# Centring v through its weights: group means on VectorE, and transposes in place of the gated layer's centring products

## The chip, the cores and the metric

The kernel runs on one core of a Trainium2 chip. The metric is the device time of one execution in microseconds (us); the median of several timed runs is given. One further execution was recorded by the hardware profiler, and all rows below come from that one. In the rows PE is TensorE's matmul, PEld its weight load, DVE is VectorE, ACT ScalarE, POOL GpSimd and SP SyncE; L258 is line 258 of the kernel.

## The reference, cut to what matters

A trunk of two layers over 1024 positions with width 1024, all in float32. The first layer multiplies the normalised input h by one wide matrix `e_w_in` and cuts the product into pieces for two mixers, an RWKV-7 time mixing and a chunked spatial gate. The change touches the gate's v alone, which is normalised over each group of 64 columns:

```python
def layernorm(x, g, b, eps):
    mu = jnp.mean(x, axis=-1, keepdims=True)
    var = jnp.mean(jnp.square(x - mu), axis=-1, keepdims=True)
    return (x - mu) * lax.rsqrt(var + eps) * g + b

v = layernorm(v.reshape(bsz, t_len, B_GROUPS, B_GROUP_DIM), ...)   # 8 groups of 64
...
mixed = jnp.einsum('gts,bcsgd->bctgd', w, v) + b_s...              # causal w, chunks of 128
return u * mixed.reshape(bsz, t_len, B_WIDTH)
```

The second layer is a sliding-window attention; a final normalisation follows.

## The kernel before

The wide matrix is walked in column blocks of 128, 25 of them after four that are done at the start, in the order of the list `ORDER`: 21, 5, 1, 9, **17**, 6, 2, 10, 22, 13, 25, 7, 3, 11, 23, **18**, 14, 26, 24, **19**, 15, 27, **20**, 16, 28. Columns 17 to 20 are v. Each column is computed for two halves of 512 positions by `gproj`, with float32 split in two parts: 8 blocks of the inner dimension times three products, so 24 matmuls of 128x512 for a half, all of tile `pproj`.

The generator `stream` does this walk. For each column it first issues the two DMAs (`wfetch`, L247, on SP's queue, 256 KB each) of the next column's weights into two of three `wraw` buffers, then the 24 matmuls of the first half, then the evacuation of that half, then `wsplit`: ScalarE rounds each raw half to `whi` (L257) and GpSimd subtracts it to `wlo` (L258); both are held behind the last matmul issued so far (`paced`). Then comes the second half.

TensorE's instructions stand in an order written out by hand: the function `drive` takes turns among several generators (scan, prep, solve, fronts, tail, ada, stream), each of which yields the latency that it expects before it wants to go on. The time mixing needs long chains that go between TensorE, ScalarE and VectorE (`solve`, `prep`, `scan`); the stream's 128x512 matmuls fill the time between. Instructions of the other engines are put in order by a scheduler from their priorities and from its own estimates of time; those of the time mixing have raised priority, those of `stream` have not. On the chip each queue runs in the order so found.

A half of v goes through `v_evac` (ScalarE copies the `pproj` result to `vT`, L992) and then through `gm_tail`: four products on TensorE, `vT` block times the constant `cblk` (identity minus 1/64 in each 64x64 block), both turn v round to positions on the partitions and take off the mean of each group of 64. ScalarE squares the result (L902), VectorE sums the squares (L904) and GpSimd takes the power -1/2 (L907); VectorE scales (L909); later come the mixing products (`mix`). Eight halves of v, two for each of the columns 17 to 20, go this way.

Of the kernel before, what the change touches and what calls it, by code (L numbers as in the profile page):

```python
# [11 lines left out]
F32 = mybir.dt.float32  # L12
# [3 lines left out]
ALU = mybir.AluOpType  # L16
AX = mybir.AxisListType
# [3 lines left out]
P = 128  # L21
# [84 lines left out]
def tile_kernel(ctx, tc, x, cons, par, rows, ada, ada0, ew, wup, sgw, sgb, ewo, ow, owo, out, dbg=None):  # L106
# [10 lines left out]
    def paced(*ops):  # L117
        for op in ops:
            behind(op, last[0])

    def cost(lhsT, rhs):
        n = math.prod(rhs.shape[1:])
        m = math.prod(lhsT.shape[1:])
        if rhs.dtype == F32R:
            return max(n if n >= 256 else 4 * n, m) / 2400.0
        return max(4 * n, 2 * m, 60) / 2400.0

    def mm(out, lhsT, rhs, **kw):
        clock[0] += cost(lhsT, rhs)
        last[0] = nc.tensor.matmul(out, lhsT=lhsT, rhs=rhs, **kw).ins  # L130

    def transpose(out, in_, ident):
        clock[0] += 512 / 2400.0
        return nc.tensor.transpose(out, in_, ident)  # L134

    V = nc.vector
# [16 lines left out]
    def pg(name):  # L153
        return ps.tile([P, HT], F32, name=name, tag="g", bufs=1)
# [12 lines left out]
    def PC(name, i):  # L167
        return prm[:, COLS[name] + i:COLS[name] + i + 1]

    ident = con[:, CONSTS["ident"]:CONSTS["ident"] + P]  # L170
    cblk = con[:, CONSTS["cblk"]:CONSTS["cblk"] + P]
# [72 lines left out]
    def wfetch(src):  # L244
        raws = [wp.tile([P, 4, P], F32, name="wraw", tag="wraw", bufs=3) for g in range(2)]
        for g in range(2):
            d = nc.sync.dma_start(out=raws[g], in_=src[:, g * 4:g * 4 + 4, :])  # L247
            if clock[0] < 100.0:
                behind(d, start_dma[0])
        return raws  # L250

    def wsplit(raws, pace=True, E=G):
        hi = wp.tile([P, KC, P], F32R, name="whi", tag="whi", bufs=2)
        lo = wp.tile([P, KC, P], F32R, name="wlo", tag="wlo", bufs=2)
        for g in range(2):
            gs = slice(g * 4, g * 4 + 4)
            a = S.activation(hi[:, gs, :], raws[g], AF.Copy)  # L257
            b = E.tensor_tensor(out=lo[:, gs, :], in0=raws[g], in1=hi[:, gs, :].bitcast(F32), op=ALU.subtract)  # L258
            if pace:
                paced(a, b)  # L260
        return hi, lo
# [14 lines left out]
    def gproj(w, half, hs=None):  # L276
        whi, wlo = w
        hhi, hlo = (hs or h)[half]
        pt = pproj("pproj")
        for k in range(KC):  # L280
            mm(pt, lhsT=whi[:, k, :], rhs=hhi[:, k, :], start=(k == 0), stop=False)
            yield 0.0
            mm(pt, lhsT=whi[:, k, :], rhs=hlo[:, k, :], start=False, stop=False)
            yield 0.0
            mm(pt, lhsT=wlo[:, k, :], rhs=hhi[:, k, :], start=False, stop=(k == KC - 1))
            yield 0.0
        return pt
# [7 lines left out]
    def new_h():  # L295
        return [new_hh(half) for half in range(2)]
# [47 lines left out]
    with tc.manual_schedule(engines={nc.tensor.engine}):  # L344
# [37 lines left out]
        def wfirst(i, g):  # L382
            raw = rt.tile([P, 4, P], F32, name="wr", tag="krv", bufs=6)
            tc.keep_in_program_order(nc.sync.dma_start(out=raw, in_=ew[FIRST[i][0]][:, g * 4:g * 4 + 4, :]))
            return raw
# [98 lines left out]
        raws = [wfirst(i, 0) for i in range(4)]  # L484
# [3 lines left out]
    with tc.manual_schedule(engines={nc.tensor.engine, nc.scalar.engine, nc.vector.engine, nc.gpsimd.engine}):  # L488
# [7 lines left out]
        raws = [wfirst(i, 1) for i in range(4)]  # L496
# [42 lines left out]
    gl = gls.enter_context(tc.tile_pool(name="gl", bufs=1, reuse_waits="tile"))  # L539
# [336 lines left out]
    def ghalf(nm, tag, bufs):  # L876
        return gl.tile([P, HT], F32, name=nm, tag=tag, bufs=bufs)

    def gm_consts(j):
        sgwt = gl.tile([P, 2, P], F32, name="sgwt", tag="sgwt", bufs=1)  # L880
        nc.scalar.dma_start(out=sgwt, in_=sgw[:, 2 * j:2 * j + 2, :])
        lnb = gl.tile([P, P], F32, name="lnb", tag="lnb", bufs=1)
        nc.scalar.dma_start(out=lnb, in_=rows[3, j * P:(j + 1) * P].partition_broadcast(P))
        bst = gl.tile([P, P], F32, name="bst", tag="bst", bufs=1)
        for g in range(2):
            nc.scalar.dma_start(out=bst[g * 64:g * 64 + 64, :], in_=sgb[2 * j + g, :].partition_broadcast(64))
        return sgwt, lnb, bst

    def gm_tail(j, half, vT):
        if half == 0:  # L890
            gmc[j] = gm_consts(j)
        sgwt, lnb, bst = gmc[j]
        yield lat("gm_tail1", 2 * j + half)
        if half == 0:
            paced(G.tensor_tensor(out=sgwt, in0=sgwt, in1=tri.unsqueeze(1).to_broadcast([P, 2, P]), op=ALU.mult))
        vn = gl.tile([P, 4, 2, 64], F32, name="vn", tag="vn", bufs=1)
        pv = pg("gvn")
        for i in range(4):
            mm(pv[:, i * P:(i + 1) * P], lhsT=vT[:, i * P:(i + 1) * P], rhs=cblk, start=True, stop=True)
        long[0] -= 1  # L900
        sq = ghalf("gsq", "gt", 3)
        S.activation(sq, pv, AF.Square)  # L902
        st = gl.tile([P, 8], F32, name="gst", tag="gst", bufs=2)
        V.tensor_reduce(out=st, in_=sq.rearrange("p (a d) -> p a d", d=64), axis=AX.X, op=ALU.add)  # L904
        V.tensor_scalar(out=st, in0=st, scalar1=1.0 / 64, scalar2=GMLP_EPS, op0=ALU.mult, op1=ALU.add)
        rs = gl.tile([P, 8], F32, name="grs", tag="grs", bufs=2)
        G.tensor_tensor(out=rs, in0=st, in1=nhalf[:, 0:8], op=ALU.pow)  # L907
        vg = vn.rearrange("p b g d -> p (b g) d")
        V.tensor_tensor(out=vg, in0=pv.rearrange("p (a d) -> p a d", d=64), in1=rs.unsqueeze(2).to_broadcast([P, 8, 64]), op=ALU.mult)  # L909
        yield lat("gm_tail2", 2 * j + half)  # L910
        yield lambda: (j, half) in gated_u
        if half == 0:
            pb = pg("lnb")
            for g in range(2):
                mm(pb[g * 64:g * 64 + 64, 0:P], lhsT=lnb[:, g * 64:g * 64 + 64], rhs=sgwt[:, g, :], start=True, stop=True)
            V.tensor_tensor(out=bst, in0=pb[:, 0:P], in1=bst, op=ALU.add)
            yield lat("lnb", 2 * j + half)
        ut = gated_u.pop((j, half))
        px = pg("mix")
        for i in range(4):  # L920
            for g in range(2):
                mm(px[g * 64:g * 64 + 64, i * P:(i + 1) * P], lhsT=vn[:, i, g, :], rhs=sgwt[:, g, :], start=True, stop=True)
        mx = ghalf("mx", "gt", 3)
        V.scalar_tensor_tensor(out=mx.rearrange("p (b t) -> p b t", t=P), in0=px.rearrange("p (b t) -> p b t", t=P), scalar=PC("sg", j), in1=bst.unsqueeze(1).to_broadcast([P, 4, P]), op0=ALU.mult, op1=ALU.add)
        V.tensor_tensor(out=ut, in0=mx, in1=ut, op=ALU.mult)
        nc.sync.dma_start(out=y0d[:, 4 + j, half * HT:(half + 1) * HT], in_=ut)
        short[0] -= 1
# [77 lines left out]

    ORDER = (21, 5, 1, 9, 17, 6, 2, 10, 22, 13, 25, 7, 3, 11, 23, 18, 14, 26, 24, 19, 15, 27, 20, 16, 28)

    def stream():
        todo = list(ORDER)
        for i in range(4):  # L1010
            if i == 1:
                raws = wfetch(ew[todo[0]])
            pt = (yield from gproj(ws[i], 1)) if i else pt1
            FIRST[i][1](1, pt)
            if i == 1:
                w = wsplit(raws)
        while todo:
            n = todo.pop(0)
            raws = wfetch(ew[todo[0]]) if todo else None
            pt = yield from gproj(w, 0)  # L1020
            yield room[n]
            evac[n](0, pt)
            if todo:
                wn = wsplit(raws)
            pt = yield from gproj(w, 1)
            yield room[n]
            evac[n](1, pt)
            if todo:
                w = wn
        done["h1"] = new_h()  # L1030

    def lat(name, un):
        return LAT.get(name, 0.0) + MORE.get(name, (0.0,) * 8)[un]
# [110 lines left out]
    def out0_thread():  # L1144
# [19 lines left out]
        for b in range(NB):  # L1164
# [22 lines left out]
            if b == NB - 2:  # L1187
# [8 lines left out]
    wes = ExitStack()  # L1196
    threads = [[0, scan_thread(), 0.0, None], [1, prep_thread(), 0.0, None], [1, solve_thread(), 0.0, None], [2, fronts_thread(), 0.0, None],
               [4, tail_thread(), 0.0, None], [5, ada_thread(), 0.0, None], [6, stream(), 0.0, None], [5, wo0_thread(), 0.0, None], [7, out0_thread(), 0.0, None]]

    def drive():  # L1200
# [191 lines left out]
    for n in range(2):  # L1392
        hi, lo = new_hh(n)
        for k in range(KC):
            raw = wp.tile([P, HT], F32, name="wraw", tag="wraw", bufs=3)
# [112 lines left out]
```

## Time and profile before

| what | value |
|---|---|
| median of 3 runs | 1091.95 us (1091.01 to 1092.3) |
| the profiled execution, its own time | 1086.66 us |
| its span, first to last instruction | 1084.8 us |
| its mean granted TensorE clock | 0.988 of full speed |
| busy: PE, PEld, DVE, ACT, POOL | 96%, 77%, 64%, 48%, 34% of the span |

The busy shares are over the whole span, which has stages with different limits: a start up to about 95 us, the first layer's mixers from about 95 to 605 us, and the first output projection and the attention layer after that. Matmuls are pipelined, so the duration of one is longer than the time that it takes up in a row of them; what one takes up is read from start to start. A row of a timeline merges neighbours of one kind (x8 is eight instructions), and what stands in brackets is the engine's idle time just before the row and what ended it.

### The profile page before, as it was taken

How to read it: one execution, taken by the hardware profiler on the slowest of the kernel's cores; microseconds unless marked ns; L12 is line 12 of the kernel's file. 1: busy time of each engine (PE TensorE's matmuls, PEld its weight loads, DVE VectorE, ACT ScalarE, POOL GpSimd, SP SyncE). 2: the span in 40 equal slices, each digit the busy share in tenths (PEclk: the TensorE clock that was granted, in tenths of full speed). 3: DMA queues.
4: the chain of work that ended last, by engine and by line, in shares of the span. 5: the costliest groups of instructions: out<-in, count | busy, mean ns of one | idle time of the engine just before them, and what ended most of it. 6: DMA issues, size and time to landing. Idle time of an engine off the chain costs nothing.

```text
span 1084.8 us, 20721 instructions
## 1 busy us (share of the span) xinstructions
PE 1039.3 (96%) x7887; PEld 834.1 (77%) x7888; DVE 694.0 (64%) x1668; ACT 521.5 (48%) x1247; POOL 370.2 (34%) x483
## 2 busy tenths in 40 slices
PE   6989989998999899999999999999999999999997
PEld 3667767777777677777888787778888888878886
DVE  4355868595868585858433688755565544488753
ACT  4464464544454546454423223336665644486521
POOL 2233323232323233233344100225455544467201
PEclk9989999999999999999999999999999999999998
DMA  9601121212121122212213655411011011251221
GB/s 363 238 18 40 60 79 59 70 50 69 64 86 57 60 68 70 69 53 84 91 61 124 184 183 177 146 45 40 23 37 40 20 40 40 98 165 59 75 81 59
DMA packets 55131, 93.42 MB, mean 86 GB/s; under 512 B 5748, under 2 KB 15988, under 8 KB 55032
## 3 DMA queue, kind: packets, MB, share of 16 engines
q1 hardware_dynamic: 45176, 77.36, 21.5%
q10 hardware_dynamic: 9856, 14.75, 4.2%
q8 instruction: 62, 1.02, 0.4%
q14 instruction: 37, 0.30, 0.1%
HBM read 79.49 MB, written 12.59 MB: 85 GB/s over the span
## 4 chain that ended last, share of the span: by engine, by line
PE 52%; DVE 4%; ACT 2%; issue 1%; DMA 1%; POOL 1%; ACTq 0%; POOLq 0%; DVEq 0%; SPq 0%
PE pproj L130 24%; PE op L130 16%; PE po L130 2%; PE pS L130 2%; PE pT L1319 2%; PE htp L134 1%; PE pM L130 1%; PE py L130 0%; DVE pr L728 0%; DMA wraw<-y0d 0%; PE mix L130 0%; DVE Sx L1305 0%; PE mq L130 0%; PE gvn L130 0%; PE uw L130 0%
## 5 line engine op out<-in xcount | busy, mean ns | idle before, releaser
L130 PE MATMUL pproj<-hi,whi 128*128 128x512 f32 x696 | 281.1, 404 | 0.7 <-ACT vt L1273 0.7
L130 PE MATMUL pproj<-hi,wlo 128*128 128x512 f32 x696 | 280.7, 403 | 0.0
L130 PE MATMUL pproj<-lo,whi 128*128 128x512 f32 x696 | 280.6, 403 | 0.0
L258 POOL TENSOR_TENSOR wlo<-wraw,whi 128x512 fp32r<-128x512 f32 x86 | 114.8, 1353 | 155.2 <-ACT whi L257 154.3
L130 PEld LDWEIGHTS pproj<-hi,whi 128*128 128x128 f32 x696 | 131.4, 189 | 27.8 <-issue 3.6
L130 PEld LDWEIGHTS pproj<-hi,wlo 128*128 128x128 f32 x696 | 131.3, 189 | 26.0 <-issue 2.4
L130 PEld LDWEIGHTS pproj<-lo,whi 128*128 128x128 f32 x696 | 131.5, 189 | 25.0 <-issue 1.7
L130 PE MATMUL op<-wo,whi 128*128 128x512 f32 x256 | 81.1, 397 | 0.1
L257 ACT ACTIVATE whi<-wraw 128x512 fp32r<-128x512 f32 x102 | 59.0, 622 | 37.2 <-issue 13.5
L1309 ACT ACTIVATE Sx<-Sx,nm 128x257 f32<-128x257 f32 (+1 forms) x128 | 62.3, 489 | 27.3 <-DVE nm L1305 25.3
L1305 DVE CUSTOM_DVE_ANT_0 Sx<-pS,bias,nsink 128x256 f32<-128x256 f32 (+1 forms) x128 | 53.5, 463 | 30.0 <-PE pS L130 28.6
L1313 POOL TENSOR_SCALAR Sx<-Sx,rc 128x256 f32<-128x256 f32 (+1 forms) x128 | 60.8, 492 | 25.6 <-DVE rc L1311 23.1
L1325 DVE TENSOR_TENSOR PL<-pT,PH 128x512 fp32r<-128x512 f32 (+1 forms) x64 | 41.6, 655 | 29.7 <-ACT PH L1324 29.2
L944 DVE SCALAR_TENSOR_TENSOR adacc<-araw,cond,adacc 128x512 f32<-128x512 f32 x56 | 48.4, 864 | 19.2 <-DMA araw<-ada 19.1
L130 PEld LDWEIGHTS op<-wo,whi 128*128 128x128 f32 x256 | 47.6, 188 | 11.4 <-ACT whi L257 0.6
L130 PE MATMUL op<-hi,yh 128*128 128x512 f32 (+1 forms) x136 | 51.8, 381 | 0.4 <-ACT yh L1423 0.4
L130 PE MATMUL op<-hi,yl 128*128 128x512 f32 (+1 forms) x136 | 51.7, 380 | 0.4 <-DVE yl L1424 0.4
L130 PE MATMUL op<-lo,yh 128*128 128x512 f32 (+1 forms) x136 | 51.5, 379 | 0.0
L130 PE MATMUL op<-wo,wlo 128*128 128x512 f32 x128 | 50.8, 397 | 0.0
L1324 ACT ACTIVATE PH<-pT 128x512 fp32r<-128x512 f32 (+1 forms) x64 | 35.7, 563 | 17.4 <-PE pT L1319 16.1
L728 DVE TENSOR_TENSOR pr<-Lf,LT 128x2 f32<-128x2 f32 (+14 forms) x120 | 42.2, 352 | 2.4
L225 POOL TENSOR_TENSOR st<-st,nhalf 128x1 f32<-128x1 f32 x16 | 9.6, 601 | 96.7 <-DVE st L224 96.7
(317 smaller groups left out, 2153.2 us busy)
## 6 DMA issues: line engine op xcount, KB each, us to landing
araw<-ada SPq DMA_DIRECT2D x64, 256.0 KB, 2.7
wraw<-ew SPq DMA_DIRECT2D x50, 256.0 KB, 3.0
wraw<-ow SPq DMA_DIRECT2D x36, 256.0 KB, 2.7
adaraw<-ada SPq DMA_DIRECT2D x16, 512.0 KB, 8.4
x<-x SPq DMA_DIRECT2D x8, 512.0 KB, 9.7
woraw<-ewo SPq DMA_DIRECT2D x16, 256.0 KB, 2.9
xr<-x ACTq DMA_DIRECT2D x16, 256.0 KB, 3.8
wraw<-y0d SPq DMA_DIRECT2D x16, 256.0 KB, 3.4
```

What stands on the lines that cost most here:

```text
L130: last[0] = nc.tensor.matmul(out, lhsT=lhsT, rhs=rhs, **kw).ins
L134: return nc.tensor.transpose(out, in_, ident)
L257: a = S.activation(hi[:, gs, :], raws[g], AF.Copy)
L258: b = E.tensor_tensor(out=lo[:, gs, :], in0=raws[g], in1=hi[:, gs, :].bitcast(F32), op=ALU.subtract)
L728: V.tensor_tensor(out=pr[:, 0:nc_, 0:i + 1], in0=Lf[:, i:i + 1, 0:i + 1].to_broadcast([P, nc_, i + 1]), in1=LTt[:, 0:nc_, 0:i + 1], op=ALU ...
L944: op = V.scalar_tensor_tensor(out=acc, in0=raw, scalar=cond[:, k:k + 1], in1=acc, op0=ALU.mult, op1=ALU.add)
L1305: V.tensor_tensor_reduce(out=Sx[:, e, off:2 * P], in0=pS3[:, e, 0:nk], in1=bias[e][:, off:], scale=1.0, scalar=nsink[:, hd:hd + 1], op0=AL ...
L1309: S.activation(pr[:, e, off:2 * P + 1], Sx[:, e, off:2 * P + 1], AF.Exp, bias=nm[:, e:e + 1], scale=-1.0, accum_out=sm[:, e:e + 1])
L1313: G.tensor_scalar(out=pr[:, e, off:2 * P], in0=pr[:, e, off:2 * P], scalar1=rc[:, e:e + 1], scalar2=0.5, op0=ALU.mult, op1=ALU.mult)
L1319: nc.tensor.transpose(pT4[:, kb, e, :], pr[:, e, kb * P:(kb + 1) * P], ident)
L1324: S.activation(PH[:, ks, :], pT2[:, ks, :], AF.Copy)
L1325: V.tensor_tensor(out=PL[:, ks, :], in0=pT2[:, ks, :], in1=PH[:, ks, :].bitcast(F32), op=ALU.subtract)
```

## The change

The mean is taken off the weights in place of the product. The four products of a half become four transposes against the identity. For columns 17 to 20 a new function runs on VectorE over the two raw weight tiles before they are split: for each partition and inner block it sums each group of 64 columns, and subtracts a 64th of that sum in place.

```diff
         for i in range(4):
-            mm(pv[:, i * P:(i + 1) * P], lhsT=vT[:, i * P:(i + 1) * P], rhs=cblk, start=True, stop=True)
+            transpose(pv[:, i * P:(i + 1) * P], vT[:, i * P:(i + 1) * P], ident)
         long[0] -= 1
...
+    def wcentre(n, raws):
+        if 17 <= n < 21:
+            for raw in raws:
+                rg = raw.rearrange("p k (b d) -> p (k b) d", d=64)
+                wm = gl.tile([P, 8], F32, name="wm", tag="wm", bufs=2)
+                V.tensor_reduce(out=wm, in_=rg, axis=AX.X, op=ALU.add)
+                V.scalar_tensor_tensor(out=rg, in0=wm.unsqueeze(2).to_broadcast([P, 8, 64]), scalar=-1.0 / 64, in1=rg, op0=ALU.mult, op1=ALU.add)
+
     def stream():
...
             evac[n](0, pt)
             if todo:
+                wcentre(todo[0], raws)
                 wn = wsplit(raws)
```

`transpose` and `mm` add the same time to `drive`'s clock for a 128x128 float32 block (512/2400 us); `transpose` does not set the matmul behind which `paced` instructions are held. The two new VectorE instructions are not `paced`.

## Rows read from the trace of the kernel before

**Rows 1.** The page: busy time of the engines with its share of the span, and PE's busy share in 40 equal slices of the span (tenths).
```profile
PE 1039.3 (96%) x7887; PEld 834.1 (77%) x7888; DVE 694.0 (64%) x1668; ACT 521.5 (48%) x1247; POOL 370.2 (34%) x483
...
PE   6989989998999899999999999999999999999997
```

**Rows 2.** The page: the chain that ended last, by engine.
```profile
PE 52%; DVE 4%; ACT 2%; issue 1%; DMA 1%; POOL 1%; ACTq 0%; POOLq 0%; DVEq 0%; SPq 0%
```

**Rows 3.** Windows: stretch, its length, then busy time (and instructions) of PE, PEld, DVE, ACT and POOL, granted clock, DMA share, GB/s. The first layer's mixers, and the stretch in which column 18's weights are split.
```profile
95.00:605.00 510.00, 488.71 (x5048) 383.69 (x5048) 346.11 (x801) 243.45 (x552) 165.50 (x135) 0.99 0.23 72
...
385.00:410.00 25.00, 23.82 (x188) 18.51 (x188) 24.00 (x62) 10.94 (x22) 11.80 (x10) 1.00 0.29 86
```

**Rows 4.** The waits of PE between 95 and 605 us, longest first: engine, tile, line, releaser: us in total, times, longest.
```profile
PE pM L130 <- DVE Tq L760: 5.6, 2, 2.9
PE chain L130 <- DVE PA L838: 5.6, 7, 1.7
PE pM L130 <- ACT M L752: 5.6, 3, 2.6
```

**Rows 5.** PE's timeline around the first centring products (`gvn`) and around four transposes (`kb`) a little later: start, us, engine, line, operation.
```profile
182.20 0.39 PE L130 MATMUL pproj<-hi,wlo 128*128 128x512 f32 x1
182.43 1.05 PE L130 MATMUL gvn<-con,vT 128*128 128x128 f32 x8
183.24 0.48 PE L130 MATMUL pproj<-hi,whi 128*128 128x512 f32 x1
...
184.48 0.39 PE L130 MATMUL pproj<-hi,wlo 128*128 128x512 f32 x1
184.72 0.60 PE L134 MATMUL kb<-con,sqk 128*128 128x128 f32 x4
185.07 0.48 PE L130 MATMUL pproj<-hi,whi 128*128 128x512 f32 x1
```

**Rows 6.** Windows, columns as in rows 3: the stretch of rows 5, and one of the stretches at half clock.
```profile
181.00:188.00 7.00, 7.00 (x42) 6.04 (x41) 6.73 (x15) 1.51 (x4) 5.64 (x4) 1.00 0.26 77
195.30:198.70 3.40, 3.40 (x30) 2.47 (x30) 2.40 (x5) 1.83 (x5) 0.00 (x0) 0.50 0.25 77
```

**Rows 7.** Groups of DVE instructions by line and shape: count, then busy us and mean ns of one, then idle time before them.
```profile
L565 DVE TENSOR_REDUCE nsk<-sqk 128x8 f32<-128x512 f32 x8 | 5.5, 683 | 0.1
...
L867 DVE SCALAR_TENSOR_TENSOR bv<-yc,der,bv 128x512 f32<-128x512 f32 x8 | 6.0, 752 | 15.0 <-ACT yc L866 15.0
...
L944 DVE SCALAR_TENSOR_TENSOR adacc<-araw,cond,adacc 128x512 f32<-128x512 f32 x56 | 48.4, 864 | 19.2 <-DMA araw<-ada 19.1
```

**Rows 8.** Timelines of POOL and ACT: the split (`wlo`) of columns 18 and 19, and the evacuation of the first half of each of these columns (`vT`).
```profile
402.46 2.99 POOL L258 TENSOR_TENSOR wlo<-wraw,whi 128x512 fp32r<-128x512 f32 x2
...
498.91 2.53 POOL L258 TENSOR_TENSOR wlo<-wraw,whi 128x512 fp32r<-128x512 f32 x2
...
427.89 0.60 ACT L992 ACTIVATE vT<-pproj 128x512 f32<-128x512 f32 x1
...
517.54 0.60 ACT L992 ACTIVATE vT<-pproj 128x512 f32<-128x512 f32 x1 [0.18 <-PE pproj L130]
```

**Rows 9.** DMA issues of weight columns between 95 and 605 us (KB each, median us to landing), and from SP's timeline the issues of the raw weights of columns 17, 18, 19 and, with one of the next column, 20.
```profile
wraw<-ew SPq DMA_DIRECT2D x45, 256.0 KB, 3.0
...
135.60 0.86 SPq L247 DMA_DIRECT2D wraw<-ew  x2
...
387.94 1.61 SPq L247 DMA_DIRECT2D wraw<-ew  x2
...
471.46 2.84 SPq L247 DMA_DIRECT2D wraw<-ew  x2
...
534.95 11.85 SPq L247 DMA_DIRECT2D wraw<-ew  x3
```

**Rows 10.** Timelines of DVE and PE where column 17's raw weights land.
```profile
140.04 0.75 DVE L314 SCALAR_TENSOR_TENSOR krv<-pproj,prm,krv 128x511 f32<-128x511 f32 x1
...
142.86 0.29 DVE L758 TENSOR_TENSOR Zq<-Zq,pM 128x128 f32<-128x128 f32 x1 [0.64 <-issue]
...
143.79 0.45 DVE L760 STREAM_TRANSPOSE Tq<-Zq 128x256 f32<-128x256 f32 x1
...
142.02 0.73 PE L130 MATMUL pM<-Zq,M 32*32 32x16 f32 x64 [2.60 <-ACT M L752]
...
144.86 0.69 PE L130 MATMUL pM<-Tq,N 32*32 32x32 f32 x32
```

**Rows 11.** Timelines of DVE and PE after column 18's raw weights have landed.
```profile
408.88 0.42 DVE L733 TENSOR_TENSOR ZT<-Tm,rcon 128x256 f32<-128x256 f32 x1
...
413.21 0.69 DVE L621 SCALAR_TENSOR_TENSOR BK<-kkn,tha 64x512 f32<-64x512 f32 x1
416.16 0.75 DVE L867 SCALAR_TENSOR_TENSOR bv<-yc,der,bv 128x512 f32<-128x512 f32 x1 [2.26 <-ACT yc L866]
...
411.73 0.75 PE L130 MATMUL pM<-ZT,Dg 16*32 16x32 f32 x64
...
416.35 0.60 PE L134 MATMUL bkt<-con,BK 128*128 128x128 f32 x4
```

**Rows 12.** DVE's timeline: the first instructions after its idle times behind the landings of columns 19 and 20.
```profile
486.49 0.86 DVE L814 TENSOR_TENSOR Z<-mq,i 64x256 f32<-64x256 f32 x2 [4.76 <-PE mq L130]
...
548.21 0.28 DVE L838 SCALAR_TENSOR_TENSOR PA<-chain,dC,PA 128x64 f32<-128x64 f32 x1 [5.83 <-PE chain L130]
```

## The prediction

> **What bounds the kernel now.** I read first the busy times and the slices of the page: PE is busy 96% of the span, in nearly every slice nine tenths or more, DVE 64% [rows 1]. The chain that ended last has PE with 52%, DVE with 4% [rows 2] (its shares don't fill the span; I take only the order from it). Then the windows: in the 510 us of the first layer's mixers, where the whole change lies, PE is busy 488.71 us and DVE 346.11 us [rows 3]. So PE's idle time there is about 21 us, and what is taken from PE's own work shortens the kernel unless a wait takes its place. PE's waits in that stage show which waits there are: three kinds of 5.6 us each, all in the chains of the time mixing, on DVE's `Tq`, on DVE's `PA` and on ACT's `M` [rows 4]. No wait for `whi` or `wlo` is among the nine that the view lists. So DVE work is cheap where DVE is idle, and it is on PE's path where it stands in front of `Tq`, `PA` or what ACT needs for `M`.
>
> **What the change takes away.** A float32 product of 128x128 is two matmul instructions, a transpose one: the four products of a half are x8, the four transposes of `kb` x4 [rows 5]. What they take up is read from start to start: `gvn` starts at 182.43 and the next `pproj` at 183.24, 0.81 us; `kb` starts at 184.72 and the next `pproj` at 185.07, 0.35 us. From the `pproj` before to the one behind it is 1.04 against 0.59 us, which gives the same difference. Of the same shapes and in the same surroundings a half gains 0.46 us, and eight halves 3.7 us (8 x 0.46 = 3.68). The order on PE should stay, since the hand-written clock counts both alike. A small part could be lost where PE then waits 0.46 us longer for something that doesn't move; with 21 of 510 us idle [rows 3] that is seldom, so I deduct nothing here and let the stalls below stand for it.
>
> [...]
>
> **What it adds.** Eight sums over 128x512 and eight fused multiply-adds over 128x512 on DVE, no DMA and nothing on another engine. The nearest sum takes 0.683 us, the nearest multiply-add from SBUF 0.752 us; one that runs much beside other traffic 0.864 us [rows 7]. A column is two of each: 2 x (0.683 + 0.752) = 2.9 us, at most 3.1 us; four columns 11.5 to 12.4 us. If it all lay on PE's path the change would cost 11.5 - 3.7 = 7.8 us; if none did it would give 3.7 us. Column by column:
>
> - **Splitting later.** `whi` now waits for DVE, and `wlo` behind it. Columns 18 and 19 have their `wlo` done at 405.45 and 501.44, and their first half is evacuated at 427.89 and 517.54 [rows 8]: 22 and 16 us, of which the 24 matmuls of the half take 24 x 0.233 (the spacing of `pproj` in rows 5) = 5.6 us and the interleaved work some more. 3.1 us fits in. What is queued behind a waiting `whi` on ACT are evacuations and the chain's `M` and `Z`; I take zero for it, since the raw weights are there well ahead of the split (column 18's at about 392.5, its `wlo` at 402.46 [rows 8, 9]), and leave what it could do to the slow rival.
> - **Where the sums will stand.** They are not held behind a matmul as the split is, so a scheduler that fills gaps will put them as soon as the raw weights are there: 3.0 us after an issue [rows 9], so at 138.6 to 139.5 us for column 17, 391 to 392.5 for 18, 474.5 to 477 for 19, and from about 538 for 20.
> - **Columns 19 and 20.** DVE is idle 4.76 us before 486.49 and 5.83 us before 548.21 [rows 12]. 2.9 us fit into either: zero, or 2.9 us if they stand ahead of a link of the chain instead.
> - **Column 17.** Right where its weights land, DVE has `krv` at 140.04, then `Zq` (0.64 us idle before it) and `Tq`, which ends at 144.24; PE already waits 2.60 us for ACT's `M` at 142.02, and takes `Tq` at 144.86 [rows 10]. A sum ahead of `Zq` delays `Tq`, whose slack is 0.62 us. Bounds: nothing if all four instructions come behind `Tq`, 2.9 us if all come ahead. The two raw tiles land a microsecond apart, so I expect one instruction to slip ahead: 0.7 us.
> - **Column 18.** DVE is busy 24.00 of the 25 us from 385 to 410 [rows 3], and there the sums push all that follows. `ZT` ends at 409.30 and PE takes it at 411.73; `BK` ends at 413.90 and PE takes it at 416.35 [rows 11]. The slack is 2.43 and 2.45 us, against 2.9 to 3.1: a stall of 0.4 to 0.7 us, of which I take 0.5. Behind that DVE has 2.26 us idle before 416.16 [rows 11], so the delay ends there. Bounds: nothing if they are put behind it, 2.9 us if they find no slack.
>
> **The sum.** -3.7 + 0.7 + 0.5 = -2.5 us. The profiled execution took 1086.66 us, 5.3 us below the median of the runs; the terms are differences inside one execution, so the median moves by as much: 1091.95 - 2.5 = 1089.5 us. Between no stall and 1.5 us of stalls this case runs from 1088.2 to 1089.8 us. A measurement of this kernel tells about 0.2%, that is 2.2 us, from no change; the sum is just beyond it.
>
> **The rivals.**
>
> - **The gain is eaten.** One column's DVE time comes through whole (2.9 us at column 17 or 18), or stalls of 1.5 to 5.9 us in all: -2.2 to +2.2 us, its middle 1091.2 us (-3.7 + 2.9). For it: PE's waits on `Tq`, `PA` and `M` stand close to both landings [rows 4, 10]. Against it: half of the columns meet idle DVE [rows 12].
> - **Slower: VectorE's queue in front of the time mixing.** A sum that is placed ahead of a chain link holds the whole queue, also while it waits for the second raw tile: of column 19's two issues the second comes up to 2.84 us after the first [rows 9]. At 2.9 us for each of columns 17, 18 and 19 it is 8.7 - 3.7 = +5.0 us, 1097.0 us. It decides from 3.7 + 2.2 = 5.9 us of stalls, that is from two columns at full price. Against it: the chains have the higher priority.
> - **The clock falls at the transposes.** A stretch at half clock is 3.4 us at 0.50 [rows 6]; it does 1.7 us of work and so loses 1.7 us. One costs half the gain; two with the 1.2 us of stalls give -3.7 + 3.4 + 1.2 = +0.9 us, 1092.9 us. [...]
> - **More than the sum.** The chains move against the clock's windows, no column stalls, and one stretch at half clock goes: -3.7 - 1.7 = -5.4 us, 1086.6 us.
> - **That the change doesn't do what it says**: that a transpose here takes up as much as a product; the 0.35 us of `kb` [rows 5] leaves next to no room for this, and I count it with the eaten gain.
>
> **How the numbers follow.** The forecast has 42 in 100, the eaten gain 28, slower 18, more than the sum 8, the clock 4. Faster by over 0.2% are the first and the fourth, 50 in 100; within 0.2% the second and the last, 32; slower 18. The range from 1086.5 to 1095.0 us holds all but most of the slow case. The forecast's own range is 1088.2 to 1089.8 us.
>
> **What would show it.** Each `gvn` group should be x4 and take about 0.35 us to the next `pproj`. Right for the costs: a DVE group of eight sums at 0.68 us and eight multiply-adds at 0.75 to 0.86 us; no PE wait on `whi` or `wlo`; PE's wait before the `pM` of 142 us grown by less than a microsecond. It is wrong if the waits of PE on `Tq`, `PA` or `M` grow by more than 1.5 us in all, if ACT waits for DVE at `whi` in front of an evacuation, or if there are more or fewer stretches at half clock than before.

## The result and the profile after

The change made the kernel slower. The median went from 1091.48 us (1090.88 to 1092.3, 4 runs) to 1097.21 us (1096.61 to 1098.73, 4 runs), a ratio of 1.0049 with a 95% interval from 1.003 to 1.0067. The forecast was 1089.5 us, its range ended at 1095.0 us. The profiled execution of after took 1096.61 us. Three of the kernels below had one execution each of 1544.75 to 1677.46 us, at a granted clock of 0.555 to 0.598, which every number here leaves out.

The busy times of the page, then the windows of the first layer's mixers and of the stretch in which column 18 is split (columns as in rows 3), both of after:

```profile
PE 1042.1 (95%) x7856; PEld 833.6 (76%) x7856; DVE 702.1 (64%) x1684; ACT 521.5 (48%) x1247; POOL 369.9 (34%) x483
```

```profile
95.00:605.00 510.00, 483.91 (x4958) 378.20 (x4957) 348.19 (x806) 239.07 (x544) 161.69 (x133) 0.97 0.22 69
385.00:410.00 25.00, 23.71 (x216) 17.48 (x213) 22.18 (x58) 10.97 (x26) 3.60 (x4) 1.00 0.19 54
```

PE is busy 4.8 us less in the same 510 us than in [rows 3] although the work takes longer: it waits more. The granted clock of the stretch is 0.97 where it was 0.99. PE's waits between 95 and 615 us in after, longest first:

```profile
PE pM L130 <- DVE Tq L760: 6.7, 4, 2.9
PE pM L130 <- DVE ZT L733: 6.0, 3, 2.9
PE chain L130 <- DVE PA L838: 4.4, 7, 1.7
PE pM L130 <- ACT N L711: 2.7, 8, 1.0
PE pM L130 <- ACT M L752: 2.3, 2, 1.5
PE pproj L130 <- DVE krv L314: 1.6, 1, 1.6
```

There is no wait on `krv` in before, and for `ZT` one of 0.3 us:

```profile
PE pM L130 <- DVE ZT L733: 0.3, 1, 0.3
```

That on `M` has shrunk from the 5.6 us of [rows 4]; at 190 us `ZT` has taken its place. The gain itself is there. PE's timeline of after at the first centring group:

```profile
184.41 0.39 PE L130 MATMUL pproj<-hi,wlo 128*128 128x512 f32 x1
184.64 0.60 PE L134 MATMUL gvn<-con,vT 128*128 128x128 f32 x4
184.99 0.48 PE L130 MATMUL pproj<-hi,whi 128*128 128x512 f32 x1
```

From `gvn` to the next `pproj` is 0.35 us, where it was 0.81 [rows 5]. When the starts of the same PE instructions in both traces are set side by side, after is 2.1 us ahead at 132 us, 1.7 us behind at 144.86, 6.1 us behind at 192 and 8.4 to 10.9 us behind from 266 us on (times of before). At each of the eight `gvn` groups it catches up by 0.4 to 0.5 us. So most of the loss arises before 270 us, and only its first part where a sum was added.

**The first place** is column 17. DVE's timeline of after, and PE's waits there:

```profile
124.38 0.23 DVE L728 TENSOR_TENSOR pr<-Lf,LT 128x45 f32<-128x45 f32 x1
125.70 0.69 DVE L1013 TENSOR_REDUCE wm<-wraw 128x8 f32<-128x512 f32 x1 [1.09 <-DMA wraw<-ew]
126.30 0.68 DVE L569 TENSOR_TENSOR sqk<-kt,nik 128x512 f32<-128x512 f32 x1
126.90 0.19 DVE L729 TENSOR_REDUCE LT<-pr 128x5 f32<-128x45 f32 x1
...
127.99 1.77 DVE L1014 SCALAR_TENSOR_TENSOR wraw<-wm,wraw 128x512 f32<-128x512 f32 x1
129.68 0.25 DVE L728 TENSOR_TENSOR pr<-Lf,LT 128x50 f32<-128x50 f32 x1
...
133.48 0.50 PE L130 MATMUL pproj<-hi,whi 128*128 128x512 f32 x1 [1.57 <-DVE krv L314]
137.58 0.75 PE L130 MATMUL pM<-ZT,Dg 16*32 16x32 f32 x64 [1.53 <-DVE ZT L733]
```

The first sum is in DVE's queue between two links of the `pr`, `LT` chain that leads to `ZT`, and holds the queue 1.09 us for its raw weights; the multiply-add behind it takes 1.77 us. PE waits 1.57 us for `krv` and 1.53 us for `ZT`.

**The second place** is at 190 us, where no sum is near. DVE's timeline of after, then of the kernel before:

```profile
189.12 0.68 DVE L904 TENSOR_REDUCE gst<-gsq 128x8 f32<-128x512 f32 x1
189.72 0.27 DVE L729 TENSOR_REDUCE LT<-pr 128x8 f32<-128x128 f32 x1
189.91 0.74 DVE L944 SCALAR_TENSOR_TENSOR adacc<-araw,cond,adacc 128x512 f32<-128x512 f32 x1
...
190.65 0.70 DVE L731 STREAM_TRANSPOSE Tm<-LT 128x256 f32<-128x256 f32 x1
191.24 0.64 DVE L632 SCALAR_TENSOR_TENSOR AR<-kkn,E 128x504 f32<-128x504 f32 x1
...
192.56 1.67 DVE L621 SCALAR_TENSOR_TENSOR BK<-kkn,tha 64x512 f32<-64x512 f32 x1
194.26 0.42 DVE L733 TENSOR_TENSOR ZT<-Tm,rcon 128x256 f32<-128x256 f32 x1
...
194.74 1.08 PE L130 MATMUL pM<-ZT,Dg 16*32 16x32 f32 x64 [2.88 <-DVE ZT L733]
```

```profile
186.62 0.28 DVE L729 TENSOR_REDUCE LT<-pr 128x8 f32<-128x128 f32 x1
186.94 0.71 DVE L731 STREAM_TRANSPOSE Tm<-LT 128x256 f32<-128x256 f32 x1
187.55 0.64 DVE L904 TENSOR_REDUCE gst<-gsq 128x8 f32<-128x512 f32 x1
188.11 0.41 DVE L733 TENSOR_TENSOR ZT<-Tm,rcon 128x256 f32<-128x256 f32 x1
```

The queue has another order: `gst` and `adacc` now stand ahead of `Tm`, and `AR` and both `BK` ahead of `ZT`. From the last `LT` to the start of `ZT` it was 1.5 us and is 4.5 us, and PE waits 2.88 us for `ZT`.

**The third part** is the clock. Windows of after, columns as in rows 3: two stretches at half clock, the first behind the late `krv` and `ZT`, the second around the late `ZT`, and between them the stretch that holds the first `gvn`:

```profile
139.50:146.30 6.80, 6.04 (x80) 4.53 (x79) 4.79 (x10) 3.27 (x8) 1.27 (x1) 0.50 0.15 42
...
182.00:188.00 6.00, 6.00 (x48) 5.05 (x45) 5.76 (x14) 2.69 (x5) 5.53 (x6) 1.00 0.37 126
194.10:200.90 6.80, 6.16 (x142) 5.14 (x142) 3.20 (x8) 2.80 (x7) 1.34 (x1) 0.50 0.14 41
```

In the mixers the profiled execution of before has three stretches at half clock, 10.2 us together; after has five, 30.7 us. In these stretches of after the starts of two `pproj` matmuls lie 0.43 us apart in the median, outside them 0.23 us. Half of the difference, 10.2 us, is the most that they can cost by this estimate. With 5.3 us more of waits and 3.7 us of gain that makes up to 11.8 us. At 601 us the two traces stand 10.6 us further apart than at 132 us, and 1.6 us more are lost from there to 645 us. These two executions lie further apart than the medians, since runs of one kernel differ by several microseconds with the clock that they get (before on one chip: 1084.1 us at 0.992, 1092.2 us at 0.986).

### The profile page after: what moved, and what is told of

The parts are those of the page before. It is cut to its first block, busy times and chain, and to the rows that moved or that the text cites. A ratio compares the mean times of both kernels' runs of the same rounds, so it can differ in the third digit from the quotient of the medians.

```text
span 1094.8 us, 20680 instructions
## 1 busy us (share of the span) xinstructions
PE 1042.1 (95%) x7856; PEld 833.6 (76%) x7856; DVE 702.1 (64%) x1684; ACT 521.5 (48%) x1247; POOL 369.9 (34%) x483
## 4 chain that ended last, share of the span: by engine, by line
PE 51%; DVE 3%; DMA 2%; issue 2%; ACT 1%; POOL 0%; POOLq 0%; ACTq 0%; DVEq 0%
PE pproj L130 26%; PE op L130 14%; PE pS L130 2%; PE po L130 2%; PE pT L1328 2%; DMA araw<-ada 1%; PE py L130 1%; DMA gateb<-rows 1%; PE htp L134 1%; PE mix L130 0%; PE pM L130 0%; PE chain L130 0%; DMA wraw<-ew 0%; PE adag L130 0%; ACT Dg L710 0%
```

## The experiments

For each kernel the ratio is against runs of the kernel before on the same chip (medians of those between 1088.2 and 1090.3 us); it is not the quotient of the two medians, from which it differs by up to 0.0014. Two theories stood at the start: **A**, the sums are the cost; **B**, the transposes give VectorE's queue another order, and that is the cost; with a third, **C**, that the clock falls at the transposes.

**The kernel before, profiled again.**

> The kernel before, unchanged, profiled once more: its first profile took 1086.66 us where its timed runs take 1091.5. Between 95 and 610 us that profile has three stretches at half clock of 3.4 us each. If the difference of 4.8 us to the timed runs is the clock, this profile takes about 1091 us with two to four stretches more (each loses 1.7 us) and the same waits of PE, some 21 us. If it is not the clock, it has three stretches again and other waits.

It took 1089.13 us. PE's waits in the mixers came to 21.1 us (20.7 in the first trace), the stretches at half clock to 17.1 us instead of 10.2, at the same three places (194, 252 and 474 us). The waits repeat; the length of a stretch does not.

**The transposes without the sums.**

```diff
             if todo:
-                wcentre(todo[0], raws)
                 wn = wsplit(raws)
```

> Only the transposes; the sums over the weights are left out, so v's mean is not taken off. Theory A (the sums on VectorE stand in front of the time mixing at column 17 and are the whole cost): -3.7 us, about 1087.8 us, no wait of PE above 1.5 us near 190. Theory B (the transposes too change the order of VectorE's queue, which puts ZT behind four other instructions near 190 us): a wait of PE for ZT of about 2.9 us near 190, where before it waited 1.4 us for M, and -2.2 us or less gain, 1089 to 1092 us. [...]

1094.74 us, ratio 1.0061 (1.0037 to 1.0085). Without a single sum the kernel is as slow as after. Theory A, that the sums are the whole cost, falls.

**The sums without the transposes.**

```diff
-            transpose(pv[:, i * P:(i + 1) * P], vT[:, i * P:(i + 1) * P], ident)
+            mm(pv[:, i * P:(i + 1) * P], lhsT=vT[:, i * P:(i + 1) * P], rhs=cblk, start=True, stop=True)
```

> Only the sums over the weights; the centring products on TensorE stay. Theory A: the whole cost without the gain, 5.7 + 3.7 = 9.4 us slower, about 1101 us, and PE waits of 1.5 us for krv and for ZT between 130 and 140. Theory B: these waits, but not the one near 190, so 3 to 7 us slower, 1094.5 to 1098.5 us. Theory C: no more half-clock stretches than in the kernel before, and at most 3 us slower.

1091.1 us, ratio 1.003 (1.0011 to 1.0049). The sums do cost something, at column 17: PE's waits there are those of after, 1.57 us on `krv` and 1.53 us on `ZT`. At column 20 a wait of 1.1 us on `AR` is new.

**The sums held behind PE's work.**

```diff
-                V.tensor_reduce(out=wm, in_=rg, axis=AX.X, op=ALU.add)
-                V.scalar_tensor_tensor(out=rg, in0=wm.unsqueeze(2).to_broadcast([P, 8, 64]), scalar=-1.0 / 64, in1=rg, op0=ALU.mult, op1=ALU.add)
+                s1 = V.tensor_reduce(out=wm, in_=rg, axis=AX.X, op=ALU.add)
+                s2 = V.scalar_tensor_tensor(out=rg, in0=wm.unsqueeze(2).to_broadcast([P, 8, 64]), scalar=-1.0 / 64, in1=rg, op0=ALU.mult, op1=ALU.add)
+                paced(s1, s2)
```

> The whole change, but the sums are held behind the last matmul as the split is, so that column 17's stand where VectorE is idle (behind L815 near 157 us) and not in front of krv and ZT. Theory A: the cost goes, -2.5 to -3.7 us, 1087.8 to 1089 us. Theory B: the waits at 133 and 137 us go, the one for ZT near 190 stays: 1089.5 to 1093 us. Theory C: as slow as the change, about 1097 us.

1101.19 us, ratio 1.0122 (1.0096 to 1.0148): worse than any of the three theories had forecast. The waits at column 17 went, others came: `N` 1.68 us at 162.9, `ZT` 2.88 at 194.2, 1.55 at 364.9 and 1.20 at 423.7. To hold a few instructions back gave the rest of the queue yet another order.

**The transposes with VectorE's old order, and the order alone.** Beside the transposes only 40 of VectorE's 1668 instructions stand elsewhere, 4 on ScalarE, 1 on GpSimd, 1 transfer on SyncE and none on TensorE. A list of places and a chain of order edges put VectorE's queue back, up to the end of the mixers (the first kernel leaves out the sums, too); the same chain with the other list gives the kernel before the order that the transposes bring.

```diff
+    place = {n: i for i, n in enumerate(DVE_ORDER)}
+    seq = sorted(range(len(V.ops)), key=lambda i: place[i])
+    for a, b in zip(seq, seq[1:]):
+        behind(V.ops[b], V.ops[a].ins)
```

> Only the transposes, as in e1_transposes (v's mean is not taken off), but VectorE's whole queue up to the end of the mixers is put in the order that it has in the kernel before, by ordering hints that cost no wait on the chip. Theory B (the new order of VectorE's queue costs, not the transposes): PE's wait of 2.9 us for ZT near 194 us goes back to 1.5 us for M, PE's waits between 95 and 615 us add up to 20 to 22 us, and the time is 3.7 us below the kernel before, -2.5 to -5 us. [...]

> The kernel before with its products, but VectorE's queue in the order that e1_transposes has. Theory B: the order alone brings the wait of 2.9 us for ZT near 194 us, PE's waits of 24 us or more and more stretches at half clock: +5 to +10 us. Theory C: within 2 us of the kernel before, since there are no new transposes.

The transposes in VectorE's old order: 1091.56 us, ratio 1.0021 (1.0001 to 1.0042). The products in the new order: 1095.21 us, ratio 1.0034 (1.0016 to 1.0052). One row of PE's timeline in the latter, a kernel that has neither a transpose nor a sum of the change:

```profile
192.55 0.75 PE L132 MATMUL pM<-ZT,Dg 16*32 16x32 f32 x64 [3.13 <-DVE ZT L146]
```

The wait of after at 190 us is there without the change's instructions. ScalarE's and GpSimd's queues follow: the trace of this kernel has 4 and 1 instructions elsewhere than before, as many as with the transposes. So B holds in the main: an order of the queues, VectorE's above all, makes the kernel slower without the change. But B's forecasts were both missed: 5 to 10 us more for the order alone, and 2.5 to 5 us less with VectorE's order put back, where the gain did not appear.

**The whole change with its sums at idle places, and after again.** The same chain in after; the four instructions of column 17 stand behind an `adacc` that ended before 155 us, of 19 behind `uT` at 482, of 20 behind `PA` at 542.

> The whole change, with VectorE's queue in the order of the kernel before and the sixteen new instructions at set places: column 17's behind the adacc before 154.9 us, 19's behind the uT at 481.7 us, 20's behind the PA at 542.4 us, where VectorE was idle, 18's where e2_sums had them. Theory B: -2.5 to -3.7 us and PE's waits 20 to 23 us. Theory A (the sums cost wherever they stand): slower than e4_order by 3 us or more. Theory C: +3 to +8 us.

> The change once more, beside the others on one chip: +4 to +9 us, with five or so stretches at half clock in the mixers if these belong to it, and with three or so if those of its first profile were chance.

1094.95 us, ratio 1.0036 (1.0015 to 1.0056), and for after itself 1097.83 us, ratio 1.0058 (1.0039 to 1.0077). B had forecast 2.5 to 3.7 us less for the first, and is missed once more; 4.1 us more by mean times lies in the range of C.

**All queues put back.** Now the queues of ScalarE and GpSimd get their old order too:

```diff
+    for E, order in ((V, DVE_ORDER), (S, ACT_ORDER), (G, POOL_ORDER)):
+        if order:
+            place = {n: i for i, n in enumerate(order)}
+            seq = sorted(range(len(E.ops)), key=lambda i: place[i])
+            for a, b in zip(seq, seq[1:]):
+                behind(E.ops[b], E.ops[a].ins)
```

> The transposes in place of the products, without the sums (so the mean is not taken off v), and with the queues of VectorE, ScalarE and GpSimd all put back in the order that the kernel before has; TensorE's own order is the same in all kernels. The only difference left is the eight groups of four. Theory: the order of the queues is what cost the 6 us of the transposes alone, and what the other two queues still held differently is what kept the version with only VectorE's order restored from the gain: then no new wait of over 1 us in the mixers, 8 x 0.45 = 3.6 us less, ratio 0.9967 (0.995 to 0.998). Rival: the earlier arrival at the next waits, or a half-clock stretch more, eats the 3.6 us whatever the order: ratio 1.000 to 1.002.

> The same kernel as the transposes with all queues restored (without the sums, so the mean is not taken off v), timed again beside the products issued twice. It came out at 1.0015 with an interval that just holds no change. Theory: the 3.6 us are taken back by waits that TensorE now reaches earlier (Tq at 252 us, the chain at 337, mq at 538, wo at 603 and 625, xr at 695), so 0.999 to 1.0025 again. Rival: that result was chance and the gain is there: 0.9975 or less.

> The whole change, with the queues of ScalarE and GpSimd in the order of the kernel before, VectorE's too, and the sixteen sums set into it where VectorE stands idle (column 17 behind the adacc that ends before 155 us, 19 behind a uT at 482, 20 behind a PA at 542; 18 where the sums alone had it). Theory: the gain of 3.6 us less at most 1 us for sums that now stand in idle time: ratio 0.997 (0.995 to 0.999), a version faster than both. Rival: the sums keep a cost of their own, 2.7 us as in the kernel with sums alone: ratio 0.999 to 1.001 if the transposes then gain, 1.003 if they do not.

The transposes with every queue as before: 1091.21 us, ratio 1.0015 (0.9997 to 1.0033), and again 1090.45 us, 1.0022 (1.0007 to 1.0038). With the sums: 1090.8 us, 1.0026 (1.001 to 1.0042). Eight groups that take 3.6 us less, and nothing else, give nothing: the first forecast (0.995 to 0.998) is missed, and its rival came. Where the time goes can be seen against the second trace of before. The lead that they gain stands at the end of the mixers, 3.2 us at 603 us (1.7 us of it from one stretch at half clock fewer), and is 1.1 us at 708 us. PE's waits on the way, from the timeline of the first of these kernels:

```profile
252.15 1.07 PE L134 MATMUL pM<-Tq,N 32*32 32x32 f32 x32 [3.28 <-DVE Tq L148]
...
537.62 1.60 PE L134 MATMUL mq<-BR,PA 64*64 64x128 f32 x22 [0.97 <-ACT SV L148]
...
603.51 0.74 PE L134 MATMUL op<-wo,whi 128*128 128x512 f32 x2 [0.71 <-ACT whi L148]
...
694.66 0.66 PE L138 MATMUL htp<-con,xr 128*128 128x128 f32 x4 [0.30 <-DVE xr L148]
695.65 0.65 PE L138 MATMUL htp<-con,xr 128*128 128x128 f32 x4 [0.34 <-DVE xr L148]
```

and what held `whi`, from ScalarE's timeline:

```profile
602.83 0.63 ACT L148 ACTIVATE whi<-wraw 128x512 fp32r<-128x512 f32 x1 [3.34 <-DMA wraw<-y0d]
```

In the second trace of before the wait on `Tq` is shorter:

```profile
252.51 1.06 PE L130 MATMUL pM<-Tq,N 32*32 32x32 f32 x32 [2.95 <-DVE Tq L760]
```

It is 3.28 us where it was 2.95: PE comes earlier, `Tq` does not. `SV` and `whi` are waits that this trace of before does not have; `whi` waits for a transfer. The windows of the mixers show the same in sum, here the second trace of before, the transposes with every queue as before, and, from further down, transposes added to the products:

```profile
95.00:605.00 510.00, 488.31 (x5031) 383.25 (x5030) 343.99 (x795) 240.26 (x546) 164.62 (x135) 0.98 0.23 71
95.00:605.00 510.00, 485.85 (x5006) 379.69 (x5006) 344.65 (x798) 241.66 (x548) 164.68 (x135) 0.99 0.23 72
95.00:605.00 510.00, 489.67 (x5077) 384.89 (x5075) 344.71 (x798) 242.18 (x550) 166.16 (x135) 0.99 0.23 71
```

So PE is idle 21.7 us (21.3 in the first trace of before), 24.2 us with less work (23.0 in the second timing) and 20.3 us with more.

**The price of TensorE's time at these places.** Each product issued twice, by a call that the hand-written clock doesn't count; and two products of the projection left out behind each group, by the estimate as much time as the transposes save; both with all queues in the order of before:

```diff
             mm(pv[:, i * P:(i + 1) * P], lhsT=vT[:, i * P:(i + 1) * P], rhs=cblk, start=True, stop=True)
+            nc.tensor.matmul(pv[:, i * P:(i + 1) * P], lhsT=vT[:, i * P:(i + 1) * P], rhs=cblk, start=True, stop=True)
```

```diff
-            mm(pt, lhsT=whi[:, k, :], rhs=hlo[:, k, :], start=False, stop=False)
+            if skip[0] and k:
+                skip[0] -= 1
+                clock[0] += cost(whi[:, k, :], hlo[:, k, :])
+            else:
+                mm(pt, lhsT=whi[:, k, :], rhs=hlo[:, k, :], start=False, stop=False)
...
+        skip[0] = 2
```

> The kernel before with each of the 32 centring products issued twice in a row into the same place (the second overwrites the first with the same numbers), the queues of VectorE, ScalarE and GpSimd held in the order of the kernel before, and TensorE's order the same. It adds to TensorE what the change takes off, nearly doubled: four products take 0.81 us, so 8 x 0.81 = 6.5 us more. It prices 1 us of TensorE's time at these eight places. If such time counts in full, 6.5 us more, ratio 1.006 (1.005 to 1.007), and the 3.6 us that the transposes give back should have shown. If the waits for other engines and the transfers behind these places set the end as much, as in the version with all queues restored, where the time lost nothing, some of it is absorbed: 1.5 to 4.5 us more, ratio 1.0015 to 1.004.

> The kernel before with its centring products kept and, right behind each group of them, two products of the projection (the lo part by whi, 0.23 us each) left out, so that the projections are a little less exact; 8 x 2 x 0.23 = 3.7 us off TensorE at the same places as the transposes take it off, all queues in the order of before. If the time taken away is what brings the clock down and the waits up, this does what the transposes with restored queues did: ratio 1.0005 to 1.0025, clock 0.0007 to 0.0026 below. If the transposes are to blame, the clock is that of before, and the time between no change and the whole gain: ratio 0.9965 to 1.0003.

The products twice: 1092.07 us, ratio 1.0028 (1.001 to 1.0045), so 3.0 us more by the ratio, 4.1 by the mean times below; the estimate of the work was 6.5 us, and in the trace each group takes 0.89 us more, 7.1 us in all. 3.7 us less, without one transpose: 1089.85 us, ratio 1.001 (0.9998 to 1.0023), so no gain shows. Time taken away at these places brings nothing, by transposes or without them.

**The clock.** Transposes added in front of the products, with all queues in the order of before, and both kernels of the new order once more, on one chip:

```diff
         for i in range(4):
+            nc.tensor.transpose(pv[:, i * P:(i + 1) * P], vT[:, i * P:(i + 1) * P], ident)
             mm(pv[:, i * P:(i + 1) * P], lhsT=vT[:, i * P:(i + 1) * P], rhs=cblk, start=True, stop=True)
```

> The kernel before with the 32 transposes of vT added in front of the 32 products, into the same place, which the products then overwrite; all queues held in the order of the kernel before. TensorE gets 8 x 0.35 = 2.8 us more. If transposes bring the clock down by themselves, the mean granted clock is 0.0016 to 0.0026 below that of before beside it, and the time is 1.7 to 2.8 us longer for that and 1 to 2.8 us for the work: ratio 1.0025 to 1.005. If they do not, the clock is that of before (within 0.001) as with the products issued twice, and the work costs what it did there, 0.6 of its time: +1.7 us, ratio 1.0005 to 1.0025.

> The kernel before, products and all, with VectorE's queue in the order that the transposes give it, timed again. Order alone: 1.0034 again (1.0015 to 1.005), with a clock within 0.0015 of before's and about 5 us more at equal clock.

> The transposes without the sums (the mean is not taken off v), timed again beside the order alone: the same order, the transposes in place of the products. If the transposes bring the clock down: 1.005 to 1.007 again, and a clock 0.002 to 0.006 below that of the order alone. If that was chance: the order's cost less the gain, 1.000 to 1.003, at the clock of the order alone.

Ratios: both 1.0033 (1.0015 to 1.0051), the order alone 1.0064 (1.0039 to 1.0089), the transposes in that order 1.0059 (1.0041 to 1.0077). So in the new order too no gain of the transposes on the products shows, though an interval this wide doesn't exclude one. The added transposes take 0.44 us a group in the trace, 3.5 us in all, not the 2.8 us of the estimate.

What the clock has to do with it is read from the runs of a kernel, less those of before beside it: mean time, mean granted clock of the span, and the mean of their product, which I take as an estimate of the time at the full clock (standard errors of these differences: 0.6 to 1.4 us for the time, 0.0008 to 0.0017 for the clock, 0.4 to 0.9 us for the product). "Old order" means all queues as before.

| kernel | time, us | clock | time x clock, us |
|---|---|---|---|
| new order, products | +4.3; again +6.9 | +0.0010; -0.0037 | +5.4; +2.8 |
| new order, transposes | +5.7; again +6.9 | -0.0045; -0.0059 | +0.7; +0.4 |
| old order, transposes | +1.5; again +2.4 | -0.0007; -0.0026 | +0.7; -0.4 |
| old order, less projection | +1.4 | -0.0036 | -2.5 |
| old order, products twice | +4.1 | -0.0001 | +3.9 |
| old order, both | +3.5 | -0.0011 | +2.3 |
| sums, products | +3.1 | -0.0008 | +2.2 |
| after | +7.1 | -0.0047 | +1.8 |
| VectorE's old order, transposes | +2.2 | -0.0004 | +1.8 |
| VectorE's old order, whole change | +4.1 | -0.0023 | +1.5 |
| old order, whole change | +1.8 | -0.0004 | +1.4 |
| sums held behind PE's work | +13.0 | -0.0073 | +4.8 |

In each of the five pairs of one order where TensorE has less to do (transposes for products, or less projection) the clock is lower, by 0.0007 to 0.0055 (the largest between two chips; three of the five by more than twice their error), and 0.001 of clock is 1.1 us. What less work for PE saves at full clock, from nothing (0.7 us more) to 4.7 us, goes back in this way, by the same estimate. With VectorE's order alone put back the clock falls by 0.0004 (transposes) and 0.0023 (whole change), and the time is longer at full clock too, by 1.8 and 1.5 us. Work that is added leaves the clock within 0.0011.

Theory C, that transposes as such lower the clock, is not shown, and not excluded. Against it: less projection lowers the clock by 0.0036 without one transpose, and 32 transposes more move it by 0.0011, which is as much as its error. For it: the transposes in the new order met C's forecast (1.005 to 1.007, the clock 0.0022 below that of the order alone, with an error of 0.0020), and the ratio of both together, 1.0033, lies in C's range. The order alone missed its own forecast of the clock, which fell by 0.0037.

One rival stands untested: the kernel before with the chain of order edges and nothing else was not run. The five timings with the chain in the old order and no sums lie 1.4 to 4.1 us above before, with 3.7 us less work on TensorE as with 6.5 us more, and a straight line through the five meets unchanged work at +2.7 us. Against a cost of the chain: in the traces of the products issued twice and of both together the queues of VectorE, ScalarE, GpSimd and SyncE are those of the kernel before, instruction for instruction, those of the sequencers too. And in the new order only the products carry the chain, and the transposes without it are still no faster. If there is such a cost, the time taken away gave 0.2 to 1.3 us of 3.6 to 3.7, and not nothing.

No version of the change was faster than the kernel before.

## Why the prediction was wrong

- **The price of a group** was right: 0.35 us for 0.81, and 0.45 us a group in the landmarks.
- **"What is taken from PE's own work shortens the kernel unless a wait takes its place", with nothing deducted**, failed. I read 21 us of idle time in 510 as few waits, and concluded that time saved seldom meets one. But the question was whether a stretch of PE's work ends in a wait for something that does not move, and the mixers have 23 waits of 0.25 us or more in the trace of before. With all queues as before the term -3.7 measured +1.5 and +2.4 us in two timings. PE's idle time in the mixers took back 1.3 to 2.9 us, followed above for `Tq` and `SV`; `whi`, behind a transfer, and `xr` follow outside. The lower mean clock took 0.7 and 2.8 us in the two timings. How the loss divides differs from run to run, and is not settled. "Eaten" was a rival at 28 in 100, but with the sums as the eater.
- **"The order on PE should stay"** was right of TensorE, and I did not ask it of the other queues. Their order comes from a scheduler with an estimated timeline of its own, and the four transposes moved 40 instructions of VectorE's queue. That order is the largest term: +4.3 and +6.9 us where I had none.
- **Column 17, 0.7 us**, was too small. I took the two issues at 135.60 [rows 9] for both of the column's raw tiles. Of its tiles the first is issued 11 us earlier: in the trace of before SP issues a `wraw` at 124.58, in after at 122.45, and after's first sum waits for it until 125.70. So the sums met the `pr`, `LT` chain, and not `Zq` and `Tq`. Between 132.05 and 144.86 (times of before) after loses 3.9 us: 1.0 us of longer waits (1.57 + 1.53 + 0.76 against 0.29 + 2.60 in before) and up to 3.4 us of half clock. Alone the sums measured +3.1 us, on top of the transposes 0.2 to 1.8 us.
- **Columns 18 to 20, 0.5 us**: about right in size. The landings of 18 and 20 were misread like that of 17: in after the first sums stand at 377.06 and 535.02, the second pair at 401.31 and 547.49. Behind those of 20 PE has one wait of 0.55 us, on `AR` at 550 us, and 1.15 us with the sums alone; at 18 no stall shows.
- **The slow rival** named 1097.0 us and the queue in front of the time mixing, which is the place, but by sums ahead of chain links in three columns; it was one column, and the order for the rest. The right time came by luck from half the right mechanism. Of the signs named ahead the first did not come: the waits on `Tq`, `PA` and `M` fell from 16.8 to 13.4 us, and `ZT` and `krv`, which no term named, took 7.6 us. The last did: five stretches at half clock where there were three.
- **The clock** was a rival by a fall at the transposes. The runs here neither show nor exclude such a fall. No stretch at half clock in the mixers begins within 9 us behind a `gvn` group (the nearest one 9.1 us behind the start of the group's last instruction in after, 12.1 us in before), after has none between 379 and 604 us though five groups lie there, and transposes added to the products cost 0.0011 of clock with as large an error. The clock did take its share, around waits: in the second timing of after its mean was 0.0047 below that of before.

In mean times the steps are: order 4.3 to 6.9, transposes in place of products in that order 0.0 to 1.3, sums on top of the transposes 0.2 to 1.4 us, together 4.5 to 9.6 us; after measured 5.7 us by medians at first and 7.1 us in the second timing. As differences of the same means they must hold its time, and show no more than the sizes. What stays open: how the loss of the gain divides between waits and clock, whether the chain of order edges has a cost, and why the mean clock was lower with less work on PE (by 0.0007 to 0.0055) while the profiled executions show the stretches at the same places; a profile is one execution, and most runs have none.

## What to carry to other kernels

Before a saving on the busiest engine is counted, follow it to the next wait on that engine: if what is waited for does not move, the saving ends there, and a busy share of 96% does not exclude it (here the wait on `Tq` at 252 us was 2.95 us and became 3.28). Where a scheduler orders the queues, an edit to one engine's instructions is an edit to all queues: compare the order of each, and test the order alone on the old instructions. For a transfer's landing go by the issues of its own buffers, not by the nearest pair.

## What the runs showed of the hardware

- In the mixers the granted clock was 0.50 for 3.4, 6.8 or 10.2 us at a time, around PE's waits. Of 66 such stretches in the mixers of 17 traces, 65 begin during or shortly after a PE wait of 1.4 us or more; of the 106 such waits 40 have no stretch. In the traces of before and after alone it is all eight stretches, from 0.7 us before the end of such a wait to 1.9 us behind it. Stretch and wait repeat from kernel to kernel at the same places (140, 194, 232, 252 to 259, 361 to 375, 472 to 484 us). The runs of one kernel went with the clock: before took 1084.1 us at 0.992 and 1092.2 us at 0.986 on one chip.
- A fused multiply-add over 128x512 on VectorE took 0.69 us in the median of eight in after (682 to 1768 ns) and 1.77 us at 127.99, while GpSimd split weights (two `wlo`, 2.98 us from 126.22, so to 129.20; the multiply-add ended at 129.76). In the five traces of kernels with the sums that were read for it, all seven that began while a GpSimd instruction ran ended 0.55 us behind its end (in after also the one at 141.10, 0.99 us long, behind a `qh` that ended at 141.55), and all others took 0.67 to 0.69 us. What holds them is not shown, and not every VectorE instruction is held: `sqk`, a product of two inputs, took its usual 0.68 us from 126.30, beside the first `wlo`. The eight took 6.9 us, 0.86 us each on the mean, the upper end of my price.
- Taking 3.6 us off an engine that is busy 96% of the time gained nothing, adding 3.5 us (by the trace) cost 3.5 us and adding 7.1 us cost 4.1 us, all against the kernel before without the chain of order edges.
